# Splitting the weights of a float32 decoder trunk 1024 columns at a time instead of 512, with slots of two halves and another count of cycles per product

## The chip, the cores and the metric

The kernel runs on one core of one Trainium2 chip. The metric is the time of one execution on the device, in microseconds (us); of several runs the median is quoted. TensorE is called PE, VectorE DVE, ScalarE ACT, GpSimd POOL and SyncE SP, as in the profile.

## The reference

Two layers of a decoder trunk over 256 tokens of width 1024, all in float32. Each layer is a half-step SwiGLU FFN, a token mixer, and another half-step FFN, each between two RMS norms; layer 0 mixes by stick-breaking attention, layer 1 by multi-head latent attention.

```python
def block(x, l, g):
    f = swiglu(rms_norm(x, g[0]), ffn_w_in[l, 0], ffn_w_out[l, 0])   # 1024 -> 2 x 2816 -> 1024
    x = x + 0.5 * rms_norm(f, g[1])
    h = rms_norm(x, g[2])
    m = stick_breaking_attention(h, ...) if l == 0 else multi_head_latent_attention(h, ...)
    x = x + rms_norm(m, g[3])
    f = swiglu(rms_norm(x, g[4]), ffn_w_in[l, 1], ffn_w_out[l, 1])
    return x + 0.5 * rms_norm(f, g[5])
```

Every weight is used once by each of two blocks of 128 tokens, and all weights come from memory once, 168 MB.

## The kernel before, in words

The 256 tokens are two blocks, b = 0 and 1. A float32 product is made of three fp32r products (`mm3`, lines 476 to 479): high part by high, high by low, low by high. So every weight is first split. SP loads it into one of four `raw` tiles of 128 x 1024 (`load`, line 329). Of each raw tile `split` (line 339) makes two pieces of 512 columns: ACT rounds the columns into `hi` (line 345), then DVE subtracts `hi` from `raw` into `lo` (line 351). The raw tile is free for the next load when the last DVE subtraction is done. `hi` and `lo` each take one slot of the pool `r`, 76 tiles of 128 x 512, which also holds the split activations.

`use` (line 585) is the work of PE on one piece for one block: three products of 128 x 512, each after a load of the 128 x 128 stationary operand. A piece is used first by block 0 and later by block 1. `project` (line 595) uses eight pieces for one 512-column result, `out_rows` (line 607) and `attn_out` (line 681) four for 256 rows of an output weight.

In an FFN the 2816 hidden columns come in 11 tiles of 256. For each tile and block, `project` gives gate and up side by side in one PSUM bank; ACT takes the silu of the gate (line 634), DVE multiplies by up (line 636, called the gate operation below), PE transposes the result (line 482), ACT and DVE split it (lines 492 and 512), and `out_rows` uses it one tile later. A round is what both blocks do for one tile: 72 products of 512 columns and four transposes.

Nothing is ordered by hand. The program records operations (`Plan.op`) with an engine, a duration and what they read and write, and `Plan.run` (line 167) emits them by a list schedule: the engine that can start first takes its next operation. PE prefers any operation of class 0 that is ready (transposes, scores, attention products); otherwise it takes block 0's next piece unless block 0 leads by `LEADS` pieces, and else block 1's. ACT may start a split only while fewer than `CAPS` pieces are held. Durations are formulas of the number of columns (lines 65 to 78). On the chip each engine runs its own instructions strictly in that order, waiting on semaphores.

```python
def pe_us(n):
    return max(n, 256) / 2400.0 + 0.0018
```

Of the kernel before, what the change touches and what calls it, by code (L numbers as in the profile page):

```python
# [19 lines left out]
P = 128  # L20
# [13 lines left out]
RD = 32  # L34
# [14 lines left out]
STOCK = 5  # L49
# [7 lines left out]
# Durations, in microseconds, by which the order of the instructions is chosen.  # L57
# [7 lines left out]
def pe_us(n):  # L65
    return max(n, 256) / 2400.0 + 0.0018
# [14 lines left out]
class Buf:  # L81
    """A tile of a pool; it takes a slot with its first operation and gives it back after its last."""
# [13 lines left out]
class Op:  # L96
    __slots__ = ("eng", "us", "fn", "cls", "deps", "users", "wait", "bufs", "ready", "end", "table", "blk", "piece", "alt", "phase")


class Plan:  # L100
    """Operations with what they read and write; run() emits them in the order of a list schedule."""

    def __init__(self, pools, set_table):
        self.free = {tag: [(0.0, i) for i in range(len(tiles))] for tag, tiles in pools.items()}
# [36 lines left out]
    def alt(self, o, eng, us, fn):  # L141
        """Another engine that may take the operation."""
        o.alt[eng] = (us, fn)

    def slots_ready(self, o):
# [5 lines left out]
        for tag, n in need.items():  # L151
            if len(self.free[tag]) < n:
                return math.inf
            w = max(w, sorted(self.free[tag])[n - 1][0])
        return w

    def bank_ready(self, o, eng):
        """Two engines never access one bank at the same time."""
# [8 lines left out]
    def run(self):  # L167
# [13 lines left out]
        while left:  # L181
# [39 lines left out]
            for b in o.bufs:  # L221
                if b.tile is None:
                    f = self.free[b.tag]
                    s_ = min(x for x in f)
                    f.remove(s_)
                    b.slot = s_[1]
                    b.tile = self.tiles[b.tag][b.slot]
# [3 lines left out]
            if o.piece is not None:  # L231
# [3 lines left out]
                elif e == "pe":  # L235
                    self.pos[o.blk] = o.piece + 1
                    if o.blk == 1:
                        self.held -= 1
            for b in o.bufs:
# [3 lines left out]
                if b.left == 0 and b.slot is not None:  # L243
                    self.free[b.tag].append((b.end + CROSS, b.slot))
# [11 lines left out]
class Piece:  # L256
    """128 rows of a weight by up to 512 of its columns: the moving operand of three matrix products."""

    def __init__(self, key, raw, off, n):
        self.key, self.raw, self.off, self.n = key, raw, off, n  # L260
        self.hi, self.lo = Buf("r"), Buf("r")
# [3 lines left out]
def trunk(ctx: ExitStack, tc: tile.TileContext, x, positions, norm_g, ffn_w_in, ffn_w_out,  # L265
# [6 lines left out]
    def T(shape, dtype, name, pool=None):  # L272
# [3 lines left out]
        "r": [T([P, 512], F32R, f"r{i}") for i in range(RSLOTS)],  # L276
# [8 lines left out]
    # ---------------------------------------------------------------- constants  # L285
# [23 lines left out]
    # The tensor engine's clock rises with use: it is kept busy until the first operands are there.  # L309
# [14 lines left out]
    # ---------------------------------------------------------------- stream of weights  # L324
# [4 lines left out]
    def load(loads):  # L329
        """loads: (view of the raw tile, source, bytes)."""  # L330
# [8 lines left out]
    def split(raw, key, off, n, ks):  # L339
        pc = Piece(key, raw, off, n)  # L340
# [4 lines left out]
        h = op("act", act_us(n), lambda: nc.scalar.copy(pc.hi[:, :n], raw[:, off:off + n]),  # L345
# [4 lines left out]
        def low():  # L350
            nc.vector.tensor_tensor(out=pc.lo[:, :n], in0=raw[:, off:off + n], in1=pc.hi[:, :n].bitcast(F32),  # L351
# [3 lines left out]
    def add(loads, parts):  # L355
        """parts: (key, offset, columns, loads it reads)."""
        raw = load(loads)
        for part in parts:
            split(raw, *part)
# [12 lines left out]
    def add_in2(kind, w, c0, c1, n):  # L372
        """[1024, n] at c0 beside [1024, n] at c1."""
        at = 2
        for h in range(KC // at):
            add([(view(0, at, 2 * n, 0, n), rows(w, h * at * P, at, c0, n), size(at, n)),
                 (view(0, at, 2 * n, n, 2 * n), rows(w, h * at * P, at, c1, n), size(at, n))],
                [(kind + (at * h + k,), k * 2 * n, 2 * n, (0, 1)) for k in range(at)])

    def add_in(kind, w, c0, n):  # L380
        for h in range(KC // 2):
            add([(view(0, 2, n), rows(w, h * 2 * P, 2, c0, n), size(2, n))],
                [(kind + (2 * h + k,), k * n, n, (0,)) for k in range(2)])

    def add_rows(kind, w, r0, by_half=False):
        raws = []
        for k in range(2):
            raws.append(load([(view(0, 1, D), rows(w, r0 + k * P, 1, 0, D), size(1, D))]))
            if not by_half:
                for n in range(2):  # L390
                    split(raws[k], kind + (k, n), n * 512, 512, (0,))
        if by_half:
            for n in range(2):
                for k in range(2):
                    split(raws[k], kind + (k, n), n * 512, 512, (0,))

    def add_ffn(l, f):
        for j in range(NJ + 1):
            if j < NJ:
                add_in2(("in", l, f, j), ffn_w_in[l, f], j * FT, FF + j * FT, FT)  # L400
            if j >= 1:
                add_rows(("out", l, f, j - 1), ffn_w_out[l, f], (j - 1) * FT, (l, f, j) == (1, 1, NJ))
# [10 lines left out]
    def add_mla():  # L413
        add_in(("mi",), mla_w_in[0], 0, MLA_IN)
        for kind, g in steps(MLA_ORDER):
            if kind == "u":
                add([(view(0, 2, NQ), rows(mla_w_uq[0], 0, 2, g * NQ, NQ), size(2, NQ))],
                    [(("uq", g, k), k * NQ, NQ, (0,)) for k in range(2)])
                add([(view(0, 1, NKV), rows(mla_w_ukv[0], 0, 1, g * NKV, NKV), size(1, NKV))],
                    [(("ukv", g), 0, NKV, (0,))])  # L420
# [3 lines left out]
    # ---------------------------------------------------------------- the tokens, and the gains of the norms  # L424
# [47 lines left out]
    # ---------------------------------------------------------------- helpers  # L472
# [664 lines left out]
```

## Time and profile before

| what | value |
|---|---|
| median of 3 runs | 970.42 us (970.26 to 970.98) |
| profiled execution, first to last instruction | 968.2 us |
| instructions | 13457 |
| PE busy | 956.9 us, 99% |
| DVE busy | 643.3 us, 66% |
| ACT busy | 562.7 us, 58% |
| DMA | 170.10 MB, mean 176 GB/s |
| splits on ACT and on DVE | 628 each |

The profiled execution's own time is known by its span; the 2.2 us by which the median of the runs is longer lie before the first and after the last instruction. A busy share says how long an engine had an instruction in it. For PE the ends are modelled, so the distance from one start to the next is the better measure of what a product costs.

### The profile page before, as it was taken

The page shows a single profiled execution, that of the slowest core. Times are in us where ns is not written, and L with a number is a line of the kernel's source. Part 1 is how long each engine was busy: PE and PEld are TensorE (multiplying, and loading weights), DVE is VectorE, ACT ScalarE, POOL GpSimd, SP SyncE. Part 2 cuts the span into 40 slices and gives each one's busy share as a digit, 9 for nine tenths or more (in the row PEclk, how much of TensorE's full clock was granted, in tenths as well). Part 3 has the DMA queues.
Part 4 walks back from the last instruction along what each step waited for, and adds up shares of the span by engine and source line. Part 5 has one row for each costly group of instructions (what it writes and reads, how often), then busy time and mean ns, then how long its engine had stood idle before and what let it go on. Part 6 is the DMA issues. An engine that isn't in the chain of part 4 may idle for free.

```text
span 968.2 us, 13457 instructions
## 1 busy us (share of the span) xinstructions
PE 956.9 (99%) x4575; PEld 797.1 (82%) x4575; DVE 643.3 (66%) x1214; ACT 562.7 (58%) x1202; POOL 26.2 (3%) x75
## 2 busy tenths in 40 slices
PE   8999999999999999999999999999999999999997
PEld 6778888888888888888888888888899988888885
DVE  7884646678777875645477564556899997555533
ACT  7754535568878764545364453545798776444421
POOL 2000000000000000000000000000200000000000
PEclk9999999999999999999999999999999999999999
DMA  8885665634434385656745656575614178666511
GB/s 276 280 249 184 193 199 184 207 131 153 131 109 153 112 276 176 193 180 188 225 131 174 190 184 192 179 232 168 192 41 131 32 236 278 196 194 188 186 62 44
DMA packets 127974, 170.10 MB, mean 176 GB/s; under 512 B 8768, under 2 KB 109472, under 8 KB 127904
## 3 DMA queue, kind: packets, MB, share of 16 engines
q1 hardware_dynamic: 127792, 169.18, 55.2%
q8 instruction: 36, 0.59, 0.3%
q14 instruction: 34, 0.28, 0.1%
q10 hardware_dynamic: 112, 0.05, 0.0%
HBM read 168.15 MB, written 1.05 MB: 175 GB/s over the span
## 4 chain that ended last, share of the span: by engine, by line
PE 92%; DMA 3%; DVE 2%; ACT 1%; issue 1%; POOL 0%; SPq 0%; DVEq 0%; POOLq 0%; ACTq 0%
PE bank L474 88%; PE bank L482 5%; DMA raw<-in_ffn_w_in_dram 3%; DVE r L351 2%; ACT r L345 1%; SPq L334 0%; DVE w L636 0%; DVE w L559 0%; ACT r L492 0%; DVE x L581 0%; DVEq L1133 0%; ACT junk L540 0%; POOLq L1133 0%; POOL cbuild L299 0%; POOL invf L818 0%
## 5 line engine op out<-in xcount | busy, mean ns | idle before, releaser
L474 PE MATMUL bank<-r,r 128*128 128x512 f32 (+3 forms) x4080 | 926.2, 384 | 0.3 <-ACT r L345 0.2
L474 PEld LDWEIGHTS bank<-r,r 128*128 128x128 f32 (+1 forms) x4080 | 736.7, 188 | 139.5 <-ACT r L345 1.2
L351 DVE TENSOR_TENSOR r<-raw,r 128x512 fp32r<-128x512 f32 (+1 forms) x628 | 400.1, 683 | 42.4 <-ACT r L345 33.1
L345 ACT CAST r<-raw 128x512 fp32r<-128x512 f32 (+1 forms) x628 | 353.9, 616 | 56.8 <-DMA raw<-in_ffn_w_in_dram 26.7
L634 ACT ACTIVATE w<-bank,rpre 128x256 f32<-128x256 f32 x88 | 41.7, 474 | 215.5 <-PE bank L474 215.4
L636 DVE SCALAR_TENSOR_TENSOR w<-bank,rpre,w 128x256 f32<-128x256 f32 x88 | 42.5, 483 | 185.9 <-ACT w L634 185.9
L492 ACT CAST r<-bank 128x256 fp32r<-128x256 f32 (+5 forms) x166 | 64.2, 399 | 75.6 <-PE bank L482 65.7
L512 DVE TENSOR_TENSOR r<-bank,r 128x256 fp32r<-128x256 f32 (+5 forms) x166 | 74.3, 454 | 45.8 <-ACT r L492 44.7
L482 PE MATMUL bank<-ident,w 128*128 128x128 f32 (+1 forms) x326 | 55.0, 272 | 2.1 <-DVE w L636 2.0
L482 PEld LDWEIGHTS bank<-ident,w 128*128 128x128 f32 (+1 forms) x326 | 41.3, 137 | 16.6 <-DVE w L636 4.0
L512 DVE TENSOR_TENSOR r<-w,r 128x512 fp32r<-128x512 f32 x48 | 32.5, 687 | 4.9 <-ACT r L507 2.0
L540 ACT ACTIVATE junk<-bank 128x512 bf16<-128x512 f32 x24 | 14.3, 597 | 22.6 <-PE bank L474 22.5
L578 DVE TENSOR_TENSOR w<-bank,w 128x512 f32<-128x512 f32 x24 | 16.4, 684 | 15.9 <-ACT junk L540 15.7
L544 POOL TENSOR_TENSOR rpost<-ms,half_neg 128x1 f32<-128x1 f32 x12 | 6.6, 548 | 700.0 <-DVE ms L542 700.0
L559 DVE TENSOR_TENSOR w<-bank,gT 128x512 f32<-128x512 f32 x24 | 16.3, 686 | 2.2 <-PE bank L482 2.0
L540 ACT ACTIVATE junk<-x 128x512 bf16<-128x512 f32 x24 | 15.1, 631 | 4.3 <-DVE x L581 2.3
L581 DVE SCALAR_TENSOR_TENSOR x<-w,rpost,x 128x512 f32<-128x512 f32 x24 | 17.1, 745 | 0.4
L482 PE MATMUL bank<-ident,x 128*128 128x128 f32 x96 | 15.0, 297 | 0.0
L482 PEld LDWEIGHTS bank<-ident,x 128*128 128x128 f32 x96 | 12.9, 155 | 1.9 <-issue 0.2
L492 ACT CAST r<-w 128x512 fp32r<-128x512 f32 x20 | 12.2, 619 | 3.6 <-DVE w L559 3.5
L1035 ACT ACTIVATE w<-bank,mx 128x128 f32<-128x128 f32 (+1 forms) x32 | 13.1, 425 | 0.4 <-DVE mx L1031 0.3
L736 DVE SCALAR_TENSOR_TENSOR w<-bank,w 128x512 f32<-128x512 f32 x12 | 8.2, 689 | 4.3 <-ACT w L734 4.1
(85 smaller groups left out, 211.5 us busy)
## 6 DMA issues: line engine op xcount, KB each, us to landing
raw<-in_ffn_w_in_dram SPq DMA_DIRECT2D x352, 256.0 KB, 3.9
raw<-in_ffn_w_out_dram SPq DMA_DIRECT2D x88, 512.0 KB, 4.3
raw<-in_sb_w_in_dram SPq DMA_DIRECT2D x32, 256.0 KB, 3.6
raw<-in_sb_w_in_dram SPq DMA_DIRECT2D x8, 512.0 KB, 4.7
raw<-in_sb_w_out_dram SPq DMA_DIRECT2D x8, 512.0 KB, 3.3
raw<-in_mla_w_out_dram SPq DMA_DIRECT2D x8, 512.0 KB, 3.9
w<-in_norm_g_dram SPq DMA_DIRECT2D x12, 256.0 KB, 4.8
raw<-in_mla_w_in_dram SPq DMA_DIRECT2D x4, 416.0 KB, 3.6
```

Source lines behind the costliest of these rows:

```text
L345: h = op("act", act_us(n), lambda: nc.scalar.copy(pc.hi[:, :n], raw[:, off:off + n]), r=rr, w=[(pc.hi, 0)], cls=1, after=splits[-1:], piece=i)
L351: nc.vector.tensor_tensor(out=pc.lo[:, :n], in0=raw[:, off:off + n], in1=pc.hi[:, :n].bitcast(F32), op=ALU.subtract)
L474: nc.tensor.matmul(o, a, b, start=start, stop=stop, skip_group_check=True)
L482: nc.tensor.transpose(o, i, ident[:])
L492: nc.scalar.copy(dst(), src())
L512: nc.vector.tensor_tensor(out=dst(), in0=src(), in1=hi().bitcast(F32), op=ALU.subtract)
L540: op("act", act_us(512, 1), lambda src=src, h=h: nc.scalar.activation(junk[:], src(), AF.Square, scale=scale, accum_out=ss[:, h:h + 1]), r ...
L559: op("dve", dve_us(512), lambda h=h, y=y, tr=tr: nc.vector.tensor_tensor(out=y[:].rearrange("p (k t) -> p k t", t=P), in0=tr[:].rearrange( ...
L578: op("dve", dve_us(512), lambda h=h, t=t: nc.vector.tensor_mul(out=t[:], in0=acc[h][:], in1=g[h][:]), r=[(acc[h], 0), (g[h], 0)], w=[(t, 0 ...
L581: op("dve", dve_us(512) + 0.06, lambda h=h, t=t: nc.vector.scalar_tensor_tensor(xt[b][h][:], t[:], k.rpost[:], xt[b][h][:], op0=ALU.mult, ...
L634: op("act", act_us(FT, 1), lambda o=o, hid=hid: nc.scalar.activation(hid[:, 0:FT], o[:, 0:FT], AF.Silu, scale=k.rpre[:]), r=[(o, 0), (k.rp ...
L636: op("dve", dve_us(FT) + 0.06, lambda o=o, hid=hid: nc.vector.scalar_tensor_tensor(hid[:, FT:], o[:, FT:], k.rpre[:], hid[:, 0:FT], op0=AL ...
```

## The change

Four things change together.

- A piece is a whole raw tile, up to 1024 columns. `split` issues one ACT and one DVE instruction where there were two of each. The keys of the pieces lose one index.
- `use` does for one block all that a piece of 1024 columns is for: six products of 512 columns instead of three. `out_rows` with `by_half` uses the two halves of a piece in two operations, and the piece counts as used by block 1 after the second (`last`).
- The pool has 38 slots `R` of 128 x 1024. A piece takes a whole slot, a split activation one half (`take`, `give`); a half is taken first where the other half is in use. The bytes are the same. `LEADS`, `CAPS` and `STOCK` are counted in the larger pieces, so they are about halved.
- The schedule counts a product of n columns as n + 32 cycles of 2.4 GHz, at least 260, where it was n cycles, at least 256, and 1.8 ns.

```diff
-LEADS = [14, 12, 9, 16, 17, 7]
-CAPS = [28, 29, 23, 22, 32, 23]
-RSLOTS = 76
+LEADS = [7, 6, 5, 8, 8, 4]
+CAPS = [14, 14, 12, 11, 16, 12]
+RSLOTS = 38
-STOCK = 5
+STOCK = 3
...
 def pe_us(n):
-    return max(n, 256) / 2400.0 + 0.0018
+    return max(n + 32, 260) / 2400.0
...
+    def take(self, b, t):
+
+        if b.tag == "R":
+            i = min((i for i, p in enumerate(self.pairs) if None not in p), key=lambda i: max(self.pairs[i]))
+            self.pairs[i] = [None, None]
+            b.slot = (i, 0, 2)
+            b.tile = self.tiles["R"][i]
+        elif b.tag == "r":
+            i, h = min(((i, h) for i, p in enumerate(self.pairs) for h in range(2) if p[h] is not None),
+                       key=lambda x: (max(self.pairs[x[0]][x[1]], t), self.pairs[x[0]][1 - x[1]] is not None,
+                                      self.pairs[x[0]][x[1]]))
...
-        "r": [T([P, 512], F32R, f"r{i}") for i in range(RSLOTS)],
+        "R": [T([P, 1024], F32R, f"r{i}") for i in range(RSLOTS)],
...
-        h = op("act", act_us(n), lambda: nc.scalar.copy(pc.hi[:, :n], raw[:, off:off + n]),
+        h = op("act", act_us(n), lambda: nc.scalar.copy(pc.hi[:, :n], raw[:, :n]),
...
-            nc.vector.tensor_tensor(out=pc.lo[:, :n], in0=raw[:, off:off + n], in1=pc.hi[:, :n].bitcast(F32),
+            nc.vector.tensor_tensor(out=pc.lo[:, :n], in0=raw[:, :n], in1=pc.hi[:, :n].bitcast(F32),
...
-                [(kind + (at * h + k,), k * 2 * n, 2 * n, (0, 1)) for k in range(at)])
+                kind + (h,), at * 2 * n)
...
-        for kc in range(KC):
-            xh, xl = k.xh[kc // 4], k.xl[kc // 4]
-            c = slice((kc % 4) * P, (kc % 4 + 1) * P)
-            use(b, key + (kc,), lambda wh, wl, xh=xh, xl=xl, c=c, kc=kc, o=o: mm3(
-                o[:, :width], xh[:, c], xl[:, c], wh, wl, kc == 0, kc == KC - 1),
-                o, [(xh, 0), (xl, 0)], width)
+        for q in range(KC // 2):
+            xh, xl = k.xh[q // 2], k.xl[q // 2]
+
+            def fn(wh, wl, xh=xh, xl=xl, q=q):
+                for i in range(2):
+                    kc = 2 * q + i
+                    c, n = slice((kc % 4) * P, (kc % 4 + 1) * P), slice(i * width, (i + 1) * width)
+                    mm3(o[:, :width], xh[:, c], xl[:, c], wh[:, n], wl[:, n], kc == 0, kc == KC - 1)
+            use(b, key + (q,), fn, [o], [(xh, 0), (xl, 0)], 6 * pe_us(width))
```

The number of instructions on PE stays: 4575 matrix instructions, of which 422 are transposes of activations. The transposes stand in 129 groups between other products before and in 121 after. Lines move: 345, 351, 474, 482, 512, 559, 636 of the kernel before are 376, 382, 494, 502, 532, 579, 664 after.

The first place is PE's order where the first weights arrive. `x` is a block of tokens, and `r` names are parts of activations and weights. Before:

```order
L474 MATMUL bank_154<-r_64,r_61 128x512
L474 MATMUL bank_154<-r_67,r_61 128x512
L474 MATMUL bank_154<-r_64,r_62 128x512
L482 MATMUL bank_155<-ident,x_189 128x128 x4
L482 MATMUL bank_156<-ident,x_189 128x128 x4
L474 MATMUL bank_154<-r_66,r_61 128x512
L474 MATMUL bank_154<-r_69,r_61 128x512
```

Now:

```order
L502 MATMUL bank_116<-ident,x_151 128x128 x4
L494 MATMUL bank_117<-r_63,r_61 128x512
L494 MATMUL bank_117<-r_65,r_61 128x512
L494 MATMUL bank_117<-r_63,r_61 128x512 x2
L494 MATMUL bank_117<-r_65,r_61 128x512
L494 MATMUL bank_117<-r_63,r_61 128x512
L502 MATMUL bank_118<-ident,x_151 128x128 x4
L494 MATMUL bank_117<-r_64,r_61 128x512
L494 MATMUL bank_117<-r_67,r_61 128x512
```

Four of the eight transposes of block 1's tokens have moved ahead of the first product, and the other four stand behind six products instead of three.

The second place is DVE's order at the same time. Lines 512 and 532 make low parts of activations, 559 and 579 multiply transposed tokens by a gain, 351 and 382 make low parts of weights. Before:

```order
L512 TENSOR_TENSOR r_62<-w_139,r_61 128x512
L512 TENSOR_TENSOR r_65<-w_140,r_63 128x512
L351 TENSOR_TENSOR r_67<-raw_146,r_64 128x512
L351 TENSOR_TENSOR r_69<-raw_146,r_66 128x512
L351 TENSOR_TENSOR r_71<-raw_147,r_68 128x512
L351 TENSOR_TENSOR r_72<-raw_147,r_70 128x512
L559 TENSOR_TENSOR w_141<-bank_155,gT 128x512
L542 TENSOR_SCALAR msx_203<-ssx_202 128x1
L559 TENSOR_TENSOR w_142<-bank_156,gT 128x512
```

Now:

```order
L532 TENSOR_TENSOR r_61<-w_101,r_61 128x512
L532 TENSOR_TENSOR r_62<-w_102,r_62 128x512
L382 TENSOR_TENSOR r_65<-raw_108,r_63 128x1024
L579 TENSOR_TENSOR w_103<-bank_116,gT 128x512
L562 TENSOR_SCALAR msx_165<-ssx_164 128x1
L382 TENSOR_TENSOR r_67<-raw_109,r_64 128x1024
L532 TENSOR_TENSOR r_66<-w_103,r_66 128x512
L579 TENSOR_TENSOR w_104<-bank_118,gT 128x512
L518 CAST r_70<-w_104 128x512
L532 TENSOR_TENSOR r_70<-w_104,r_70 128x512
```

The work on block 1's tokens now stands between the first two splits and before the third.

The third place is DVE's order at the first FFN's gate operation for the hidden tile 1 of block 0, the fourth gate operation of the program. Before:

```order
L351 TENSOR_TENSOR r_77<-raw_148,r_72 128x512
L351 TENSOR_TENSOR r_78<-raw_148,r_74 128x512
L636 SCALAR_TENSOR_TENSOR w_138<-bank_156,rpre_198,w_138 128x256
L351 TENSOR_TENSOR r_80<-raw_149,r_81 128x512
L351 TENSOR_TENSOR r_84<-raw_149,r_98 128x512
```

Now:

```order
L382 TENSOR_TENSOR r_68<-raw_110,r_67 128x1024
L664 SCALAR_TENSOR_TENSOR w_100<-bank_117,rpre_160,w_100 128x256
L382 TENSOR_TENSOR r_69<-raw_111,r_72 128x1024
L664 SCALAR_TENSOR_TENSOR w_101<-bank_114,rpre_166,w_101 128x256
L532 TENSOR_TENSOR r_73<-bank_119,r_73 128x256
```

The gate operation stands behind the subtraction of the same raw tile, the 19th, which is now one instruction of 1024 columns instead of two of 512.

## Rows read from the trace of the kernel before

**Rows 1.** The page of the profile: its span, and busy time by engine.

```profile
span 968.2 us, 13457 instructions
PE 956.9 (99%) x4575; PEld 797.1 (82%) x4575; DVE 643.3 (66%) x1214; ACT 562.7 (58%) x1202; POOL 26.2 (3%) x75
```

**Rows 2.** Windows by stage: length, busy us (x instructions) of each engine, clock, DMA share, GB/s.

```profile
0.00:62.66 62.66, 57.91 (x242) 44.62 (x243) 50.02 (x127) 42.88 (x84) 5.70 (x37) 1.00 0.85 273
62.66:690.00 627.34, 627.34 (x2943) 521.21 (x2944) 403.24 (x703) 359.13 (x729) 10.41 (x18) 1.00 0.57 178
690.00:800.00 110.00, 110.00 (x664) 98.66 (x663) 102.94 (x237) 89.27 (x244) 8.96 (x18) 1.00 0.40 125
```

**Rows 3.** The chain that ended last: start us, us, what; two rounds, last products.

```profile
81.54 14.99 PE bank L474 x66
...
98.36 14.99 PE bank L474 x66
...
957.03 4.80 PE bank L474 x21
```

**Rows 4.** Who waited for whom, PE: total us, times, longest.

```profile
PE bank L482 <- DVE w L636: 2.0, 3, 1.2
```

**Rows 5.** Groups by line and shape: count, busy us, mean ns, idle before and releasers.

```profile
L474 PE MATMUL bank<-r,r 128*128 128x512 f32 x3672 | 870.8, 393 | 0.3 <-ACT r L345 0.2
```

**Rows 6.** The same view, the split on ACT (line 345).

```profile
L345 ACT CAST r<-raw 128x512 fp32r<-128x512 f32 x612 | 346.5, 619 | 55.8 <-DMA raw<-in_ffn_w_in_dram 26.7 <-DMA raw<-in_ffn_w_out_dram 14.8 <-PE bank L474 8.7
...
L345 ACT CAST r<-raw 128x384 fp32r<-128x384 f32 x8 | 3.9, 511 | 1.0 <-DMA raw<-in_mla_w_uq_dram 1.0
```

**Rows 7.** The same view, the split on DVE (line 351).

```profile
L351 DVE TENSOR_TENSOR r<-raw,r 128x512 fp32r<-128x512 f32 x612 | 391.9, 686 | 41.8 <-ACT r L345 32.4 <-ACT w L731 0.6 <-PE bank L474 0.6
...
L351 DVE TENSOR_TENSOR r<-raw,r 128x384 fp32r<-128x384 f32 x8 | 4.3, 552 | 0.6 <-ACT r L345 0.6
```

**Rows 8.** Timeline of the first 23 us: start us, us, engine, line, op.

```profile
3.72 0.94 SPq L439 DMA_DIRECT2D x<-in_x_dram  x2
...
7.79 2.18 ACT L345 CAST r<-raw 128x512 fp32r<-128x512 f32 x4
8.45 2.03 PE L474 MATMUL bank<-r,r 128*128 128x512 f32 x3 [0.25 <-ACT r L345]
8.52 2.49 DVE L351 TENSOR_TENSOR r<-raw,r 128x512 fp32r<-128x512 f32 x4
...
10.28 1.91 PE L482 MATMUL bank<-ident,x 128*128 128x128 f32 x8
...
11.84 10.37 PE L474 MATMUL bank<-r,r 128*128 128x512 f32 x42
```

**Rows 9.** Loads of the tokens (line 439): time from issue to landing.

```profile
DMA to landing us min/median/max: 3.3/4.5/5.6
```

**Rows 10.** Timeline around the longest wait of PE.

```profile
42.72 1.15 ACT L345 CAST r<-raw 128x512 fp32r<-128x512 f32 x2 [1.00 <-DMA raw<-in_ffn_w_in_dram]
43.37 1.29 DVE L351 TENSOR_TENSOR r<-raw,r 128x512 fp32r<-128x512 f32 x2 [0.65 <-ACT r L345]
...
44.58 0.48 DVE L636 SCALAR_TENSOR_TENSOR w<-bank,rpre,w 128x256 f32<-128x256 f32 x1
...
45.11 0.44 PE L482 MATMUL bank<-ident,w 128*128 128x128 f32 x2 [1.16 <-DVE w L636]
```

**Rows 11.** Timeline at the start of the last FFN.

```profile
803.33 0.62 ACT L345 CAST r<-raw 128x512 fp32r<-128x512 f32 x1 [1.53 <-DMA raw<-in_ffn_w_in_dram]
...
804.59 0.48 DVE L636 SCALAR_TENSOR_TENSOR w<-bank,rpre,w 128x256 f32<-128x256 f32 x1
...
805.13 0.44 PE L482 MATMUL bank<-ident,w 128*128 128x128 f32 x2
```

**Rows 12.** Windows of the start: columns as in the windows above.

```profile
5.00:15.00 10.00, 9.74 (x34) 6.85 (x33) 8.84 (x17) 8.16 (x18) 1.78 (x3) 1.00 1.02 341
15.00:62.66 47.66, 45.68 (x204) 36.70 (x203) 40.53 (x110) 32.58 (x64) 0.00 (x0) 1.00 0.85 269
```

More of the change, by code (lines that the diff above doesn't have):

```diff
@@ L96 @@
 class Op:
-    __slots__ = ("eng", "us", "fn", "cls", "deps", "users", "wait", "bufs", "ready", "end", "table", "blk", "piece", "alt", "phase")
+    __slots__ = ("eng", "us", "fn", "cls", "deps", "users", "wait", "bufs", "ready", "end", "table", "blk", "piece", "alt", "phase", "last")
 class Plan:
     def __init__(self, pools, set_table):
-        self.free = {tag: [(0.0, i) for i in range(len(tiles))] for tag, tiles in pools.items()}
+        self.free = {tag: [(0.0, i) for i in range(len(tiles))] for tag, tiles in pools.items() if tag != "R"}
+        self.pairs = [[0.0, 0.0] for _ in pools["R"]]
         self.tiles = pools
@@ L222, in run @@
                 if b.tile is None:
[L223 to L227, printed above, removed]
+                    self.take(b, t)
             fn()
@@ L337, in load, with split @@
         return raw
[L339 to L340 removed]
+    def split(raw, key, n, ks):
+        pc = Piece(key)
         i = len(pieces)
@@ L350, in low, with add @@
         def low():
-            nc.vector.tensor_tensor(out=pc.lo[:, :n], in0=raw[:, off:off + n], in1=pc.hi[:, :n].bitcast(F32),
+            nc.vector.tensor_tensor(out=pc.lo[:, :n], in0=raw[:, :n], in1=pc.hi[:, :n].bitcast(F32),
                                     op=ALU.subtract)
         op("dve", dve_us(n), low, r=rr + [(pc.hi, 0)], w=[(pc.lo, 0)], cls=1)
[L355 to L359, printed above, removed]
+    def add(loads, key, n):
+        split(load(loads), key, n, range(len(loads)))
     stream, splits = [], []
@@ L382, in add_in, with add_rows @@
             add([(view(0, 2, n), rows(w, h * 2 * P, 2, c0, n), size(2, n))],
-                [(kind + (2 * h + k,), k * n, n, (0,)) for k in range(2)])
-    def add_rows(kind, w, r0, by_half=False):
-        raws = []
+                kind + (h,), 2 * n)
+    def add_rows(kind, w, r0):
         for k in range(2):
[L388 to L395, printed above, removed]
+            add([(view(0, 1, D), rows(w, r0 + k * P, 1, 0, D), size(1, D))], kind + (k,), D)
     def add_ffn(l, f):
@@ L589, in use @@
         pc = pieces[i]
-        k.last = op("pe", 3 * pe_us(n), lambda: fn(pc.hi[:, :n], pc.lo[:, :n]),
-                    r=r + [(pc.hi, 0), (pc.lo, 0)], w=[(o, 0)], cls=1, after=[k.last] if k.last else [], blk=b, piece=i)
+        k.last = op("pe", us, lambda: fn(pc.hi, pc.lo),
+                    r=r + [(pc.hi, 0), (pc.lo, 0)], w=[(q, 0) for q in o], cls=1, after=[k.last] if k.last else [],
+                    blk=b, piece=i)
         k.last.phase = phase_of[i]
+        k.last.last = last
         return k.last
```

82 lines of the change are left out of this document (52 added, 30 removed).

## The prediction

> **What bounds the kernel now.** I read the page first: PE is busy for 956.9 of 968.2 us [rows 1]. A busy share doesn't say that PE works at its pace, so I went to windows by stage [rows 2]. From 62.66 to 800 us PE has no gap at all (627.34 of 627.34 us, 110.00 of 110.00), although DVE is 94% busy in the latent attention (102.94 of 110.00). Only the first 62.66 us show idle time on PE. The chain of waits says what a product costs: 66 products of 512 columns take 14.99 us, 227.1 ns each, and a round takes 98.36 - 81.54 = 16.82 us [rows 3]. Its 72 products are 16.35 us of that. The last 21 products end at 961.8 us; the 6.4 us behind them are the final norm and the store, which the change leaves alone.
>
> So the kernel is bound by the number of products times 227 ns. The change leaves that number alone. What it can move is the little that PE waits. The list of waits names it: PE's transposes waited three times, 2.0 us in all, for the gate operation on DVE [rows 4]. All three lie before 63 us, where DMA is the supplier that comes late. The rest of the early loss is the time until the first weights arrive.
>
> **The change part by part.**
>
> *Products.* 3672 products of 128 x 512 take 870.8 us of busy time [rows 5], and they stay. Six in a row for one block run as three do: in the chain the pace is 227.1 ns whether the block changes every three products or not. Cost 0. The Trainium skill, TensorE: Matmul & The Clock Gate, section Back-to-back issue gap, gives n/2.4 + 2.5 ns, that is an estimated 215.8 ns for 512 columns; by it 66 products would take 14.2 us, and the schedule's old count would be the right one. The trace shows 14.99 us, so here the new count, n + 32 cycles, is right within 0.5 ns.
>
> *Splits.* From 384 to 512 columns ACT's split goes from 511 to 619 ns, 0.84 ns per column [rows 6], DVE's from 552 to 686 ns, 1.05 ns per column [rows 7]. Continued to 1024 columns that is 1.05 us on ACT and 1.22 us on DVE. Two of 512 columns cost 1.24 and 1.37 us, less where they overlap by some 0.07 us. About 306 pairs save up to 46 us of DVE and up to 58 us of ACT, and none of it is on the path: from 62.66 us on PE never waited for either. Cost 0. What hides it is PE's own queue of products; where that cover is gone, the latency of a split counts, and that gets worse, as follows.
>
> *First weights.* Before, ACT starts the first split at 7.79 us, the first product starts at 8.45, eight transposes of block 1's tokens start at 10.28, and from 11.84 on 42 products run without a break, in 10.37 us instead of 42 x 0.227 = 9.54, because the first ones are slow [rows 8]. So six products and eight transposes are done by about 13.3 us (11.84 + 3 x 0.227 + 0.83). After, four transposes come first. They wait for block 1's first half, which is issued at 3.72 and lands at the latest 5.6 us later [rows 9], at 9.3; at 0.2 us each (1.91 us for eight) they end at 10.1. The low part is there by then (7.79 + 1.05, then 1.22, is 10.1). Six products follow, 1.36 + 0.83 us, to 12.3, and four transposes, to 13.1 or 13.3. The same work at the same time: +0.1 us, between -0.5 and +1.0.
>
> *Gate operations in the first 63 us.* Here an in-order queue decides. At the longest wait, ACT starts on a raw tile at 42.72, the moment it lands; DVE does both halves from 43.37 to 44.66; the gate operation queued behind them starts at 44.58, and the transposes at 45.11, 1.16 us late [rows 10]. The order shows the same gate operation now behind one split of 1024 columns of the same raw tile: 42.72 + 1.05 + 1.22 + 0.48 is 45.5 instead of 45.1. PE gets there after 138 products instead of 135, 0.7 us later in its own work, which takes that back if nothing else moved. But the third gate operation comes after 84 products instead of 99, some 3 us earlier, behind the 11th raw tile, whose load starts later, since work on block 1's tokens now stands ahead of DVE's second and third splits, about 2 us at the 0.69 us of 512 columns [rows 7]. PE is there at 13.2 + 78 x 0.227 + 0.4 = 31.3 us; walking the new order with the durations above puts the end of the gate operation at about 32, an estimate: a new wait of 0.7 us. The sixth stands behind one whole piece where it stood behind half of one, which adds up to 1.22 + 1.05 - 0.69 - 0.62 = 0.96 us. Lower bound: all 2.0 us vanish. Upper: each of three gains 0.96, +2.9. I take +0.5, since two of three places get later and one does not.
>
> *Start of the last FFN.* At 803.33 ACT starts on a raw tile that landed late, the gate operation follows one split of 512 columns, at 804.59, and PE's transposes start at 805.13 [rows 11]. Behind 1024 columns it would be up to 0.96 us later. Between 0 and 0.96, I take +0.4, as the new order may stand otherwise there.
>
> *Insertions.* Transposes stand in 121 groups instead of 129. A round's 16.82 us less 16.35 us of products leaves 0.47 us for four transposes in two groups [rows 3]; so a group of two costs 0.235, most of which is the transposes themselves. Eight groups fewer give at most 8 x 0.235 = 1.9 us, at least nothing. I take -0.2, as no transpose goes away.
>
> *Mixers.* The old count made PE 5% too fast (215.1 against 227.1 ns), so ACT and DVE had slack against the plan. Now the plan is exact. Lower bound 0, since DVE also loses work there; upper bound 24 chains of scores by 0.1 us, what ACT's 512 columns take (619 ns [rows 6]) beyond the 507 ns that the plan counts, +2.4. I take +0.2, because these 110 us had no gap [rows 2].
>
> Sum: 0.1 + 0.5 + 0.4 - 0.2 + 0.2 = **+1.0 us** on a span of 968.2. The median of the runs is 2.2 us above the span, which I keep: 970.4 + 1.0 = **971.4 us**. A measurement of this kernel can tell about 0.2%, 1.9 us; this is no change.
>
> **Rivals.**
>
> *DVE relieved (faster).* In the first 62.66 us DVE is busy for 50.02 us [rows 2]. Some 27 raw tiles are split there; 27 x 0.15 is 4 us less. If DVE's queue and not the landing of the weights holds the gate operations, all three waits go and the transposes' groups cost less: 970.4 - 2.0 - 0.2 = 968.2. For it: SP's raw tiles are freed by DVE. Against it: at 42.72 DVE stood idle for 0.65 us, waiting for ACT, which waited for DMA [rows 10].
>
> *Long instructions ahead of the gate (slower).* Each gate operation behind a late raw tile waits for 1024 columns. Three early ones and the one at 804 us, 0.96 us each: 970.4 + 3.8 = 974.2. It decides wherever a raw tile lands less than 1.05 + 1.22 + 0.48 = 2.75 us before PE comes to the transposes. For it: the 1.16 us above is just such a case. Against it: one place moves 0.7 us away from it.
>
> *Slower supply (slower).* Raw tiles are held through both splits. From 5 to 15 us DMA moves 341 GB/s, from 15 to 62.66 only 269 [rows 12], so something other than DMA's own rate holds it back. The Trainium skill, DMA: Bandwidth & Descriptors, section Where 436 GB/s comes from, puts the limit of one core's memory at about 358 GB/s; the 341 agree, the 269 are below it. A raw tile of 524 KB takes 1.95 us at 269 GB/s, so four slots turn in 7.8 us. Holding each 2.27 us after landing instead of 1.95 is 0.32 of 7.8, 4% of 50 us: 970.4 + 2.0 = 972.4.
>
> *Mixers stall (slower).* The upper bound above: 970.4 + 2.4 = 972.8.
>
> That the change does not do what it says is ruled out by the order: DVE has 316 splits instead of 628.
>
> **How the numbers follow.** No change, 971.4 us: 0.57. DVE relieved, 968.2: 0.14. Long instructions, 974.2: 0.17. Supply and mixers, 972.4 to 972.8: 0.12. So faster by over 0.2%: 0.14; within: 0.57; slower: 0.29. The range goes from 968.0, where the first rival stands, to 975.0, where the second does with part of another upper bound.
>
> **What would show it.** In the profile after: the pace in the chain at 227 ns; 316 splits at 1.05 us on ACT and 1.22 us on DVE; PE's waits for the gate operation between 1 and 5 us in all, still before 66 us and near 805; no idle time of PE between 66 and 690 us; the six first products done by 13.5 us. I am wrong if the split of 1024 columns costs far from 1.05 and 1.22 us, if PE idles in the mixers by more than 2.4 us, or if the round is no longer 16.8 us.

## The result and the profile after

The changed kernel takes 979.1 us, the median of 4 runs (977.48 to 980.39), beside 970.7 us for the kernel before on the same chip: a ratio of 1.0091, 95% interval 1.0075 to 1.0108. That is 8.4 us slower, outside the predicted range. The profiled execution took 980.39 us, the longest of the four, so the two profiled spans, 978.7 and 968.2 us, differ by more, 10.5 us.

The page of the profile after, as in [rows 1], span and busy time by engine:

```profile
span 978.7 us, 12800 instructions
PE 960.3 (98%) x4575; PEld 797.5 (81%) x4575; DVE 619.0 (63%) x901; ACT 534.7 (55%) x889; POOL 30.7 (3%) x75
```

DVE is relieved by 24.3 us and ACT by 28.0 us, and the kernel is slower all the same. The groups of the splits, as in [rows 6, 7]:

```profile
L376 ACT CAST r<-raw 128x1024 fp32r<-128x1024 f32 x304 | 310.9, 1049 | 65.4 <-DMA raw<-in_ffn_w_in_dram 28.6 <-DMA raw<-in_ffn_w_out_dram 19.4 <-PE bank L494 13.5
...
L382 DVE TENSOR_TENSOR r<-raw,r 128x1024 fp32r<-128x1024 f32 x304 | 363.7, 1222 | 82.4 <-ACT r L376 77.5 <-PE bank L494 3.7 <-issue 0.4
```

The chain of waits, as in [rows 3] (start us, us, what): one round is 72 products and one group of four transposes.

```profile
66.74 16.36 PE bank L494 x72
83.10 0.44 PE bank L502 x4
83.54 16.35 PE bank L494 x72
```

A product still takes 16.36 / 72 = 0.227 us, and a round 16.80 us where it took 16.82. So neither the splits' prices nor PE's pace is the loss. Windows by stage, as in [rows 2], and behind them two short windows (length, busy us and count of PE, PEld, DVE, ACT, POOL, granted clock, DMA share, GB/s):

```profile
0.00:62.66 62.66, 55.09 (x230) 41.65 (x231) 47.98 (x98) 39.12 (x53) 6.60 (x37) 0.97 0.84 266
62.66:690.00 627.34, 625.85 (x2929) 518.94 (x2928) 381.00 (x486) 338.84 (x516) 13.18 (x17) 1.00 0.57 179
690.00:800.00 110.00, 106.98 (x642) 95.34 (x641) 99.86 (x212) 85.95 (x220) 9.84 (x20) 0.98 0.35 108
...
49.00:52.30 3.30, 3.30 (x11) 2.34 (x10) 2.83 (x6) 2.62 (x4) 0.00 (x0) 0.50 0.96 306
...
708.00:711.00 3.00, 3.00 (x13) 2.72 (x12) 2.84 (x9) 2.26 (x6) 0.55 (x1) 0.50 0.00 0
```

PE has started 12 matrix instructions fewer by 62.66 us, 14 more are lost by 690 and 22 more by 800. The latent attention, which had no gap, has lost 3 us of busy time. In the two short windows PE is busy throughout at half its clock (granted 0.50, 1.2 GHz); that costs 1.65 and 1.5 us, half of each window, and shows as no wait at all.

The list of waits says for whom PE waited (total us, times, longest). Before, the only entry for a time behind the first 9 us was the one of 2.0 us [rows 4]. After, the list has, among others:

```profile
PE bank L494 <- DVE r L532: 3.5, 5, 1.6
PE bank L502 <- DVE w L664: 2.9, 2, 2.6
PE bank L502 <- DMA x<-in_x_dram: 1.6, 1, 1.6
```

The longest is the fourth gate operation, the third place of the order shown above. Its timeline:

```profile
44.91 1.05 ACT L376 CAST r<-raw 128x1024 fp32r<-128x1024 f32 x1 [0.61 <-DMA raw<-in_ffn_w_in_dram]
...
45.99 1.23 DVE L382 TENSOR_TENSOR r<-raw,r 128x1024 fp32r<-128x1024 f32 x1 [0.27 <-ACT r L376]
...
47.14 0.48 DVE L664 SCALAR_TENSOR_TENSOR w<-bank,rpre,w 128x256 f32<-128x256 f32 x1
```

The raw tile that the gate operation stands behind is taken up at 44.91 instead of 42.72 [rows 10], and the transposes start at 47.67, 2.59 us after PE was free for them. The half clock from 49 us follows this wait.

The second place is the start of the latent attention, where the low part of the compressed queries (line 532) is late:

```profile
703.36 1.68 POOL L977 TENSOR_TENSOR crs<-cms,half_neg 128x1 f32<-128x1 f32 x1 [0.91 <-DVE cms L975]
703.42 1.22 DVE L382 TENSOR_TENSOR r<-raw,r 128x1024 fp32r<-128x1024 f32 x1
...
704.44 0.47 ACT L512 CAST r<-bank 128x384 fp32r<-128x384 f32 x1
...
704.96 0.62 PE L494 MATMUL bank<-r,r 128*128 128x384 f32 x2 [0.91 <-ACT r L512]
...
705.08 0.21 DVE L979 TENSOR_SCALAR cfs<-crs,rpre 128x1 f32<-128x1 f32 x1 [0.44 <-POOL crs L977]
705.21 0.68 DVE L598 TENSOR_TENSOR w<-bank,w 128x512 f32<-128x512 f32 x1
...
705.93 0.68 DVE L598 TENSOR_TENSOR w<-bank,w 128x512 f32<-128x512 f32 x1
...
706.53 0.55 DVE L532 TENSOR_TENSOR r<-bank,r 128x384 fp32r<-128x384 f32 x1
...
707.13 1.20 PE L494 MATMUL bank<-r,r 128*128 128x384 f32 x4 [1.55 <-DVE r L532]
```

PE has already waited 0.91 us for the high part of the same queries, which ACT gave at 704.91, and then waits 1.55 us for the low part. On DVE stand, ahead of the low part, a one-column product that waits 0.44 us for POOL and two multiplications of the other block's norm (line 598), 1.3 us. (The wait for POOL is 0.44 us in the kernel before as well.) The half clock from 708 us follows this wait. In the kernel before, the same place reads:

```profile
696.56 5.14 PE L474 MATMUL bank<-r,r 128*128 128x512 f32 x24
...
698.04 0.55 DVE L512 TENSOR_TENSOR r<-bank,r 128x384 fp32r<-128x384 f32 x1
...
699.82 0.68 DVE L578 TENSOR_TENSOR w<-bank,w 128x512 f32<-128x512 f32 x1
```

There the other block was further behind. PE had 24 products to do in the meantime, and the multiplication of its norm (line 578) came 1.8 us after the low part, not ahead of it.

### The profile page after: what moved, and what is told of

It reads as the page before. It is cut to its first block, busy times and chain, and to the rows that moved or that the text cites. A ratio compares the mean times of both kernels' runs of the same rounds, so it can differ in the third digit from the quotient of the medians.

```text
span 978.7 us, 12800 instructions
## 1 busy us (share of the span) xinstructions
PE 960.3 (98%) x4575; PEld 797.5 (81%) x4575; DVE 619.0 (63%) x901; ACT 534.7 (55%) x889; POOL 30.7 (3%) x75
## 3 DMA queue, kind: packets, MB, share of 16 engines
HBM read 168.15 MB, written 1.05 MB: 173 GB/s over the span
## 4 chain that ended last, share of the span: by engine, by line
PE 91%; DVE 3%; DMA 2%; ACT 1%; issue 1%; SPq 0%; POOL 0%; DVEq 0%; POOLq 0%; ACTq 0%
PE bank L494 87%; PE bank L502 4%; DMA raw<-in_ffn_w_in_dram 2%; DVE r L382 1%; DVE r L532 1%; ACT r L376 0%; DVE w L579 0%; DVE w L598 0%; ACT junk L560 0%; DVE x L601 0%; SPq L365 0%; ACT r L512 0%; ACT junk L972 0%; POOL crs L977 0%; ACT w L1062 0%
## 5 line engine op out<-in xcount | busy, mean ns | idle before, releaser
L494 PE MATMUL bank<-r,r 128*128 128x512 f32 (+4 forms) x4063 | 927.3, 384 | 4.3 <-DVE r L532 2.9
L382 DVE TENSOR_TENSOR r<-raw,r 128x1024 fp32r<-128x1024 f32 (+3 forms) x316 | 374.2, 1209 | 88.2 <-ACT r L376 83.1
L376 ACT CAST r<-raw 128x1024 fp32r<-128x1024 f32 (+3 forms) x316 | 320.2, 1039 | 71.4 <-DMA raw<-in_ffn_w_in_dram 28.6
L560 ACT ACTIVATE junk<-x 128x512 bf16<-128x512 f32 x24 | 15.1, 628 | 10.1 <-DVE x L601 8.4
L534 DVE SCALAR_TENSOR_TENSOR r<-bank,r 64x256 fp32r<-64x256 f32 x16 | 6.8, 422 | 13.3 <-ACT r L512 11.4
```

The costliest lines, as they stand in the source:

```text
L382: nc.vector.tensor_tensor(out=pc.lo[:, :n], in0=raw[:, :n], in1=pc.hi[:, :n].bitcast(F32), op=ALU.subtract)
L494: nc.tensor.matmul(o, a, b, start=start, stop=stop, skip_group_check=True)
L560: op("act", act_us(512, 1), lambda src=src, h=h: nc.scalar.activation(junk[:], src(), AF.Square, scale=scale, accum_out=ss[:, h:h + 1]), r ...
```

## The experiments

Three theories were set against each other. **Count:** the exact count of a product took the plan's 5% slack away. **Granules:** instructions of 1024 columns and operations of six products block the in-order queues. **Constants:** the order is one draw of the list schedule; leads, caps, hold and the rest fit the order of the kernel before, and whatever moves the order draws again.

**Undoing the count, and making it alone.**

```diff
 # e1, from the changed kernel
-    return max(n + 32, 260) / 2400.0
+    return max(n, 256) / 2400.0 + 0.0018
 # e2, from the kernel before
-    return max(n, 256) / 2400.0 + 0.0018
+    return max(n + 32, 260) / 2400.0
-CAPS = [28, 29, 23, 22, 32, 23]
+CAPS = [28, 29, 23, 22, 27, 23]
 # e3, from the kernel before: the cap alone
-CAPS = [28, 29, 23, 22, 32, 23]
+CAPS = [28, 29, 23, 22, 27, 23]
 # e4, from the changed kernel
-            use(b, key + (q,), fn, [o], [(xh, 0), (xl, 0)], 6 * pe_us(width))
+                use(b, key + (q,), fn, [o], [(xh, 0), (xl, 0)], 3 * pe_us(width), i == 1)
...
```

(In e4 the output weights and the up-projection of the queries are cut into operations of three products in the same way.)

> The changed kernel with the schedule's old count of a product, max(n, 256) cycles and 1.8 ns, and all else as changed. Count theory (the exact count took away the 5% by which the plan made PE too fast, and with it the slack of ACT and DVE): most of the 8.4 us goes, 971 to 975 us, and PE's waits for the low parts of activations (5.5 us on PEld before the change of the count) fall below 2.5 us. Granules theory (instructions of 1024 columns and operations of six products block the queues): no gain, 977 to 981 us. Constants theory (the order is one draw of a list schedule whose constants were fitted to the old granules, and any change of a number draws again): somewhere between 971 and 979 us, with waits at other places.

> The kernel before, pieces of 512 columns, with the new count of n + 32 cycles. With the cap of 32 held pieces in the latent attention the list schedule runs out of slots, so the cap there is 27. Count theory: 2 to 6 us slower than the same kernel with the old count and cap 27, and waits of PE for ACT and DVE appear in the mixers. Granules theory: no difference from it beyond 1 us.

> The kernel before, whose only edit is the cap of 27 held pieces in the latent attention instead of 32: the control of the run before. Count and granules theories: within 1 us of 970.7, since neither the count nor the granules move. Constants theory: 2 to 4 us slower though nothing of the change is in it, 972.5 to 975 us, by waits of PE between 700 and 800 us that the kernel before did not have.

> The changed kernel with the work of PE on a piece in two operations of three products, as before the change; splits of 1024 columns and the new count stay. Granules theory, as far as PE's operations are meant: 973 to 976 us, and the wait of 2.7 us at 44.7 us goes. Count theory: 977 to 980 us. Constants theory: 974 to 980 us with the waits at other places.

Measured, against the kernel before: e1 974.88 us (1.0047, 1.0034 to 1.0060), e2 977.85 us (1.0077, 1.0065 to 1.0089), e3 974.51 us (1.0040, 1.0028 to 1.0053), e4 980.14 us (1.0101, 1.0088 to 1.0114). Undoing the six products in one operation gains nothing, and the wait at the fourth gate operation stays (2.43 us, now at 46.5). The old count gives 4.2 us back (979.1 to 974.88), and the new count alone costs 3.3 us (974.51 to 977.85). But the control e3, which has nothing of the change in it, is itself 4.2 us slower than the kernel before, so a difference of that size between two single orders, or the lack of one, proves no mechanism. The profile of e3, window and waits:

```profile
690.00:800.00 110.00, 107.25 (x645) 94.56 (x644) 100.27 (x231) 83.74 (x231) 9.30 (x18) 1.00 0.33 105
```

```profile
PE bank L482 <- DVE w L636: 5.7, 6, 2.7
...
PE bank L474 <- ACT r L492: 1.2, 1, 1.2
```

The 110.00 us without a gap are gone by one number that only limits how many pieces may be held. Less is loaded in the latent attention (DMA share 0.33 where it was 0.40 [rows 2]), and at the start of the last FFN gate operations are late: 2.2 us of the 5.7 lie there, three waits, the longest 1.50 us at 798.56. The wait of 1.2 us for ACT stands at 782. The longest of the six, 2.75 us, stands at 37 us, in a stretch whose order is that of the kernel before; more of this below.

**A nudge, refits, and the width of DVE's instruction alone.**

```diff
 # e7, from the kernel before
-HOLD = 0.25
+HOLD = 0.27
 # e5, from the changed kernel: constants alone
-LEADS = [7, 6, 5, 8, 8, 4]
-CAPS = [14, 14, 12, 11, 16, 12]
-HOLD = 0.25
-STOCK = 3
-WARM_B = 4
-CROSS = 0.2
+LEADS = [15, 9, 11, 10, 7, 3]
+CAPS = [8, 15, 15, 16, 15, 12]
+HOLD = 0.41
+STOCK = 4
+WARM_B = 6
+CROSS = 0.26
 # e8, from the changed kernel: the same order
-            nc.vector.tensor_tensor(out=pc.lo[:, :n], in0=raw[:, :n], in1=pc.hi[:, :n].bitcast(F32),
-                                    op=ALU.subtract)
+            for c0 in range(0, n, 512):
+                c1 = min(n, c0 + 512)
+                nc.vector.tensor_tensor(out=pc.lo[:, c0:c1], in0=raw[:, c0:c1], in1=pc.hi[:, c0:c1].bitcast(F32),
+                                        op=ALU.subtract)
```

e6 has other fitted constants (leads 7, 6, 8, 11, 7, 3; caps 12, 12, 12, 17, 16, 12; hold 0.33, stock 1, cross 0.21, block 1's tokens one load later) and the count times 0.948.

> The changed kernel, splits of 1024 columns, six products per operation and the exact count as changed; only the constants of the list schedule are fitted anew (leads, caps, stock, hold, cross and the number of warm-up products), by walking each engine's queue with durations of the two traces of before and after. Constants theory: within 2 us of the kernel before, 969 to 973 us, with PE's excess between 700 and 850 us below 2.5 us where the changed kernel has 7.0. Count theory: it stays 3 us or more above the kernel before, 973.5 to 978 us, since the exact count leaves no slack whatever the constants. Granules theory: 976 to 980 us.

> The same with the count fitted too: a product is counted 5.2% too fast, (n + 32) cycles times 0.948, ACT's formula is raised by 16 ns and DVE's lowered by 5 ns. Constants theory: as the run before, 969 to 973 us. Count theory: 969 to 973 us here, and 3 us or more faster than the run before. Granules theory: 974 to 979 us.

> The kernel before, with the one constant HOLD (how long an engine waits for an operation of class 0 before it starts a split) at 0.27 instead of 0.25. Count and granules theories: within 1 us of the kernel before. Constants theory: 1.5 to 5 us slower, 972 to 975 us, although no price, no size and no limit that binds has changed.

> The changed kernel with the same order, in which each DVE subtraction of 1024 columns is issued as two of 512 right behind each other; ACT's stay whole. It costs DVE 0.1 to 0.15 us per piece. In the trace after, a one-column power on POOL that meets a subtraction of 1024 columns takes 1.46 to 1.68 us (3.73 us once), where it took 0.93 to 1.15 us beside 512 columns. Port theory (POOL waits until the DVE instruction that runs is over, and the chains of the norms wait for POOL): POOL's longest powers fall back to 1.2 us, the wait of 1.7 us at 705 us shrinks by 0.3 to 0.6 us, and the time is 0.5 to 1.5 us below the changed kernel, 977.5 to 978.5 us. Rival (the port costs nothing that is waited for): POOL's powers get shorter, and the time is the same or up to 1.5 us longer, 979 to 980.5 us.

Measured: e5 970.63 us (1.0006, 0.9995 to 1.0017), e6 969.61 us (0.9995, 0.9986 to 1.0004), e7 974.77 us (1.0050, 1.0038 to 1.0062), e8 979.99 us (1.0104, 1.0090 to 1.0118). These decide between the theories. With large pieces, six products per operation and the exact count all left as changed, refitted constants bring the kernel back to the time before (e5; one of them adds two warm-up products). And 0.02 us on one constant of the kernel before costs 4.8 us (e7). Count theory foretold at least 973.5 us for e5, granules theory 976. Against e6, count theory foretold 3 us or more between the two; it was 1.0. One detail of constants theory was missed: from 700 to 850 us e5 lost 2.95 us, where below 2.5 was expected (7.0 in the changed kernel). The windows of e5 by stage, and the latent attention of e7:

```profile
0.00:62.66 62.66, 58.59 (x253) 44.92 (x254) 43.75 (x97) 33.86 (x50) 6.63 (x37) 1.00 0.76 235
62.66:690.00 627.34, 627.33 (x2940) 520.33 (x2940) 390.50 (x497) 351.61 (x525) 12.26 (x18) 1.00 0.58 182
690.00:800.00 110.00, 109.13 (x653) 96.39 (x653) 99.28 (x211) 89.45 (x223) 12.90 (x18) 1.00 0.39 124
```

```profile
690.00:800.00 110.00, 107.94 (x647) 94.85 (x646) 99.99 (x230) 84.06 (x233) 9.30 (x18) 1.00 0.35 113
```

The wait at the start of the latent attention in e8, where the order is that of the changed kernel:

```profile
703.27 1.75 POOL L979 TENSOR_TENSOR crs<-cms,half_neg 128x1 f32<-128x1 f32 x1 [0.91 <-DVE cms L977]
703.33 1.28 DVE L384 TENSOR_TENSOR r<-raw,r 128x512 fp32r<-128x512 f32 x2
...
707.10 1.33 PE L496 MATMUL bank<-r,r 128*128 128x384 f32 x3 [1.62 <-DVE r L534]
```

At this place the run did not do what it was meant to do: POOL's power takes as long beside two subtractions of 512 columns right behind each other as beside one of 1024 (1.75 and 1.68 us), and PE's wait stays (1.62 and 1.55 us). So the port theory was not put to the test here; what speaks against it is that DVE's wait for POOL was 0.44 us in the kernel before too. What e8 shows is that narrower subtractions in the same order gain nothing in time.

**The nudge on the other side, a second fit, and narrow splits.**

```diff
 # e9, from e6
-HOLD = 0.33
+HOLD = 0.35
 # e10, from e6: another fit
-LEADS = [7, 6, 8, 11, 7, 3]
-CAPS = [12, 12, 12, 17, 16, 12]
-HOLD = 0.33
-WARM_B = 4
+LEADS = [8, 6, 8, 9, 7, 4]
+CAPS = [11, 14, 12, 17, 30, 15]
+HOLD = 0.42
+WARM_B = 6
 # e11, from the changed kernel
-        h = op("act", act_us(n), lambda: nc.scalar.copy(pc.hi[:, :n], raw[:, :n]),
+        cuts = [(0, n // 2), (n // 2, n)] if n > 512 else [(0, n)]
+        for q, (c0, c1) in enumerate(cuts):
+            h = op("act", act_us(c1 - c0), lambda c0=c0, c1=c1: nc.scalar.copy(pc.hi[:, c0:c1], raw[:, c0:c1]),
...
```

(DVE's subtraction in e11 is cut likewise, and the cap in the latent attention is 15 instead of 16. e10 also counts a product times 0.946 and DVE 2 ns longer than the plan of before.)

> The refitted kernel with the fitted count, whose only edit is HOLD 0.35 instead of 0.33. Constants theory: it loses 1.5 to 5 us against that kernel, 971 to 974.5 us, as the kernel before did when its HOLD was moved by the same 0.02; the fit belongs to one order, for either size of pieces. Granules theory: no change, 969 to 970.5 us.

> The changed kernel with another set of fitted constants (leads, caps, hold, count, warm-up products all others than in the first fit). Constants theory: again 968.5 to 971.5 us, since many sets reach the floor, and no set falls below it by more than 1 us, as PE is bound by the number of products. Count and granules theories say nothing new here.

> The changed kernel with its splits as separate operations of 512 columns on ACT and on DVE, which the list schedule places one by one; six products per operation, the exact count and the constants as changed, but for a cap of 15 held pieces instead of 16 in the latent attention, without which the schedule runs out of slots. Granules theory, as far as long instructions are meant: 971 to 975 us. Constants theory: unfitted constants again, 973 to 981 us, with waits at other places than in the changed kernel. Count theory: 977 to 981 us.

Measured: e9 973.87 us (1.0035, 1.0021 to 1.0049), e10 968.58 us (0.9984, 0.9973 to 0.9995), e11 977.93 us (1.0078, 1.0059 to 1.0097). The nudge costs the refitted kernel 4.3 us (3.9 when each is taken against its own runs of the kernel before), as it cost the kernel before 4.8. The second fit is the fastest kernel of the study, 1.8 us below the kernel before on the same chip: barely what can be told apart. Its windows:

```profile
0.00:62.66 62.66, 59.74 (x261) 46.72 (x262) 47.49 (x100) 38.78 (x54) 5.70 (x37) 1.00 0.82 264
62.66:690.00 627.34, 627.34 (x2944) 521.20 (x2943) 389.52 (x495) 347.94 (x524) 11.55 (x18) 1.00 0.57 181
690.00:800.00 110.00, 109.82 (x658) 97.57 (x657) 98.84 (x207) 90.25 (x227) 10.52 (x18) 1.00 0.39 124
```

It gains in the start, with 261 matrix instructions by 62.66 us where the kernel before had 242 and the changed kernel 230, and the latent attention is full again at a DMA share of 0.39. Narrow splits alone gave the changed kernel 1.2 us, within what two draws differ by, and not the 971 to 975 us of granules theory.

All thirteen kernels side by side (e8 has the order of the changed kernel). "Lost" is worked out from the traces: the distance from the start of each of PE's instructions to the next, less (n + 32) / 2.4 ns (260 cycles at least), summed by stage in us, each for the one execution that was profiled. It holds waits and half clock alike.

| kernel | pieces | count | constants | median us | lost to 62.66 | to 690 | to 860 |
|---|---|---|---|---|---|---|---|
| before | 512 | old | its own | 970.0 to 970.7 | 9.5 | 3.2 | 1.8 |
| e3 | 512 | old | cap moved | 974.5 | 10.4 | 3.2 | 7.1 |
| e7 | 512 | old | hold moved | 974.8 | 8.7 | 3.3 | 6.6 |
| e1 | 1024 | old | as changed | 974.9 | 8.5 | 5.2 | 6.5 |
| e9 | 1024 | x 0.948 | fit, hold moved | 973.9 | 8.5 | 4.2 | 5.3 |
| e2 | 512 | exact | cap moved | 977.9 | 9.3 | 4.3 | 10.1 |
| after | 1024 | exact | as changed | 979.1 | 12.3 | 5.5 | 7.2 |
| e4 | 1024, by three products | exact | as changed | 980.1 | 12.3 | 4.0 | 7.7 |
| e8 | 1024, low parts in two | exact | as changed | 980.0 | 12.1 | 5.6 | 7.3 |
| e11 | 1024, splits in two | exact | as changed, cap moved | 977.9 | 11.4 | 4.6 | 7.8 |
| e5 | 1024 | exact | fitted | 970.6 | 7.3 | 4.3 | 3.4 |
| e6 | 1024 | x 0.948 | fitted | 969.6 | 6.1 | 4.6 | 1.8 |
| e10 | 1024 | x 0.946 | fitted again | 968.6 | 5.5 | 3.7 | 2.6 |

Before the columns are compared, one pair shows what a single order varies by. PE, ACT and DVE of e9 run the same order as in e6 up to 234 us, and both start alike, to 0.01 us, up to the second product. Then five more products and the first eight transposes of tokens follow, e6 first:

```profile
9.96 1.43 PE L494 MATMUL bank<-r,r 128*128 128x512 f32 x5 [0.76 <-DVE r L382]
11.23 1.03 PE L502 MATMUL bank<-ident,x 128*128 128x128 f32 x8
```

```profile
9.97 2.50 PE L494 MATMUL bank<-r,r 128*128 128x512 f32 x5 [0.47 <-DVE r L382]
12.27 1.91 PE L502 MATMUL bank<-ident,x 128*128 128x128 f32 x8
```

In e9 a product of 512 columns takes 0.427 us there, as at 1.2 GHz, and the pace of 0.227 us begins at 15.7 us instead of about 10. (The window rows print a granted clock of 1.00 for both from 10 to 15 us, so it is the pace that tells.) By then it has cost e9 some 2.6 us, all of the 2.4 us by which its start lost more than that of e6, with nothing of the order in it. e3 has the order of the kernel before up to 680 us, and there too the transposes take 1.29 us in e3 and 1.91 before [rows 8]. e3 then waits 3.5 us for gate operations in the start where the kernel before waited 2.0, and the starts come to 10.4 and 9.5. The slow pace lasts to about 13 us or longer in the kernel before, e1, e8, e9 and e11, and to about 10 us at most in the other eight. So a difference of some 2 us in the first column is within what one order varies by. Late half clock is another part of the columns: stretches of granted 0.50 between 16 and 960 us, at some 1.7 us each, stand twice in the changed kernel and in e8, once in e1, e2 and e11, and nowhere else.

What follows. Rows of unfitted constants lie between 973.9 and 980.1 us, whatever the size of the pieces; rows of fitted ones between 968.6 and 970.6. Among the unfitted, the exact count stands at 977.85 or more (five kernels, two of them with one order) and a count that is too fast at 974.9 or less (four), for both sizes of pieces. So of the 8.4 us some 4 to 5 are what each move of the order without the exact count cost (3.5 to 4.8 us in e1, e3, e7 and e9), some 3 to 4 go with the exact count at constants that were not fitted to it, and nothing that was measured can be put down to the 1024 columns themselves. How the count does it stays open: from e1 to the changed kernel it costs 3.8 us in the start and 0.7 late, from e3 to e2 1.1 us less in the start, 1.1 more up to 690 and 3.0 late, of which one stretch of half clock is 1.7. So it is not one slack lost at one place, and it rests on two pairs of single orders. With fitted constants the exact count costs 1 us (e5 against e6) or 2 (against e10), where e6 and e10, with nearly the same count, differ by 1 themselves.

The fitted kernels were chosen: the constants were searched by following each engine's queue with the durations of the two traces, and only the best went to the chip. The two nudges were set beforehand and not chosen. Not measured is what the same search would bring to pieces of 512 columns. So the runs show that the change need not cost anything; they don't show what it is worth when both kernels are fitted equally well.

## Why the prediction was wrong

- *Products, cost 0: right.* 72 products in 16.36 us are 227.2 ns each. The Trainium skill, TensorE: Matmul & The Clock Gate, section Back-to-back issue gap, gives n/2.4 + 2.5 ns, an estimated 215.8 ns, but calls that the gap of an isolated product; for a stream of loads and products it has about 131 ns. The trace after agrees with neither, and the prediction rightly went by the trace before.
- *Splits, 1.05 and 1.22 us, cost 0: right in price.* They measured 1.049 and 1.222 us. "None of it is on the path" held for the work saved. DVE and ACT saved 24.3 and 28.0 us, about half of the upper bounds. A latency got longer too, as said, but e5 has the same splits and none of the loss.
- *First weights, +0.1: about right, with luck in it.* The first four transposes waited 1.62 us for the tokens, to 9.74 us, and the second four ended at 12.2 instead of 13.1; then PE waited 0.51 us for the next piece. I had priced a transpose at 0.2 us, which is the slow pace of the kernel before (1.91 us for eight). In this execution PE was at full pace from 9.74 us on. In e8, with the same order on PE, the pace was slow until past 13 us, and the same transposes ended at 14.0. The lines of the changed kernel:

```profile
9.74 0.66 PE L502 MATMUL bank<-ident,x 128*128 128x128 f32 x4 [1.62 <-DMA x<-in_x_dram]
...
11.62 0.60 PE L502 MATMUL bank<-ident,x 128*128 128x128 f32 x4
```

- *Gate operations, +0.5 (-2.0 to +2.9): missed.* The stage lost 2.8 us more, with 2.59 us of waiting for the fourth gate operation and 1.65 of half clock behind it, in place of the 1.16 us of before [rows 10]. I had two of three places late by up to 0.96 us and let the fourth cancel itself, by taking its raw tile to land at 42.72 as before. It was taken up at 44.91. The third waited 0.29 us and the sixth not at all. No term priced the half clock that a long wait brings.
- *Start of the last FFN, +0.4: the wait went.* From 800 to 860 us PE is busy throughout.
- *Insertions, -0.2: right.* A round takes 16.80 instead of 16.82 us.
- *Slower supply (a rival): not the cause.* The changed kernel moved 266 GB/s in the first 62.66 us where the kernel before moved 273, and the raw tile of the fourth gate operation came 2.2 us later. But e5 moved only 235 GB/s there and lost 7.3 us, less than either. And from 8 to 12 us the kernel before moved 372 GB/s, above the 358 that the prediction took for the limit.
- *Mixers, +0.2 (0 to +2.4): the step that failed most.* From 690 to 860 us the changed kernel lost 5.4 us more, and 2.3 in the stage ahead, in the stick-breaking attention and where layer 1 begins. Of the 5.4, 4.4 lie between 690 and 712 us, in the two waits and the half clock shown above. I named the exact count as the lever, which e1 and e2 bear out in sign, and then took +0.2 "because these 110 us had no gap". That was the wrong reading of the row. With DVE busy for 102.94 of 110.00 us, no gap on PE was no sign of room to spare: from 690 to 860 us e3 and e7 lose 5.3 and 4.8 us more than the kernel before, without any of the change.
- *No term for the order as such.* I went place by place through the few that the old trace marked as late. In each of the runs whose order moved without a new fit, late places appeared where the old trace shows nothing. The rival "long instructions ahead of the gate" had the sign and 3.8 us, but its mechanism is not the one: narrower instructions brought 1.2 us (e11) or none (e8), and e5 has the long ones and not the loss.

## What to carry to other kernels

Where a list schedule with fitted constants sets the order, a change in it is two changes: the one that is meant, and a new draw of the order. Measure a null first (one constant moved by a hair); here it cost 4 to 5 us in three runs of three (e3, e7, e9), and a change must be refitted before its own worth is read. In this kernel the stage without a gap on PE where DVE was 94% busy lost 4.8 us in e7 by 860 us, and the one where DVE was 64% busy lost 0.1. So take a full stage beside a nearly full second engine for a close fit and forecast a loss there, not nothing. And before a difference between two profiles is put down to the order, look for a stretch in which the order is the same: here the first 62.66 us differed by up to 2.4 us even so.

## What was not expected of the hardware

- A one-column power on POOL takes 0.55 us alone, 1.15 us in the chain of the latent attention before, beside a subtraction of 512 columns on DVE, and 1.68 us beside one of 1024. At 510 us of the changed kernel one took 3.73 us, across two subtractions of 1024 columns and one of 512. Two halves in direct sequence did not let it in at 703 us of e8 (1.75 us), but did at 11.84 us of the same run (0.93). The Trainium skill, SBUF — State Buffer, section SBUF: two separate sides, says that an operation of DVE with two SBUF inputs and one of POOL that reads SBUF lock each other out for a whole instruction. The trace agrees where POOL was kept out, and adds that POOL can be kept out across several DVE instructions. Here the power in the chain of the latent attention got half a us longer (1.15 to 1.68), and DVE's wait for it did not (0.44 in both).
- The granted clock fell to half for some 3 us after PE had waited 2.59 us, and again after it had waited 0.91 and 1.55 us within 3.1 us. In e8 a wait of 2.12 us was followed by it; one of 2.43 us in e4 and one of 2.75 us in e3 were not. So the same kind of wait cost some 1.7 us more than it shows, or nothing more.
- The rise to full pace at the start varies: e6 and e9 give PE the same work at the same times up to 10 us, and the pace of 0.227 us per product begins at 10 us in one and at 15.7 us in the other.
